# Hybrid decoder block on one core: half of an early query column as three rounded products, and another sequence for the first transfers

## The chip, the cores and the metric

The kernel runs on one core of a Trainium2 chip. The metric is the device time of one launch in microseconds (us). Three runs of the kernel before took 705.67, 705.79 and 706.04 us; the median is 705.79 us. The execution that the profiler recorded took 705.09 us, of which the traced span is 703.3 us.

The engines are called as in the profile: PE multiplies matrices (PEld loads its weights), DVE and ACT work element by element, POOL does small side work and issues some transfers, SP only issues transfers.

## The reference

512 tokens and 16 learned "meta" tokens, 1024 values each, go through a layer norm. One projection of 10,240 columns gives the queries, keys, values and gates of two attention branches. The first branch (8 heads) subtracts two softmaxes with a distance bias, the second (16 heads) is a stick-breaking attention. Gated and merged, they go through an output projection and a last layer norm.

```
h = layer_norm(concat(meta, x), emb_ln_g, emb_ln_b)
lam = exp(sum(lp[0] * lp[1])) - exp(sum(lp[2] * lp[3])) + lam_init
proj = h @ w_in          # q_d k_d v_d g_d q_s k_s v_s g_s m_d m_s
a = softmax(q1 k1 + bias) - lam * softmax(q2 k2 + bias)   # first branch, causal
y_d = rms_norm(a @ v_d);  y_s = stick_breaking(q_s, k_s, v_s)
y = merge(silu(g) * y, sigmoid(m + b_gate)) @ w_out
out = layer_norm(alpha * h + y)[:, 16:]
```

All inputs are float32, and what is computed must keep nearly float32 precision.

## The kernel before, in words

**Rounded products.** Most projections are not made in float32. Each operand is split into a high half (rounded to the faster type fp32r) and a low half (what the rounding lost), and a product is three matmuls into one accumulator: high by high, high by low, low by high. Activations are in `hTh` and `hTl` (transposed: feature rows, token columns; 16 meta columns, then 512). A weight column of 128 outputs is split by `hi` (a cast on ACT, L185) and `lo` (a subtraction on DVE, L190), in two pieces of four feature blocks each; the pieces live in six buffers `w2`. `HALF` names the two halves of the 512 tokens.

**The opening.** Before the high and low halves exist, the kernel loads four tiles of x (`xts`, 128 tokens each), normalizes them (`stats`, `rstd`, `norms`: DVE, POOL, one part on ACT), transposes them on PE (`turn`, L344) and scales them out of the accumulators into `hF` in float32 (`scaled`, L384 on ACT, L386 on DVE). The first two query columns (heads of units 0 and 1) are multiplied in plain float32 from `hF` (`query`, L390): column 0 token block by token block (step `x`), column 1 in two halves of 256 tokens (step `y`). Float32 matmuls need no splits, so PE has work while the splits are made. The first key column and the first value column follow as rounded products over 264 tokens at a time (`proj_pos`, L515).

**What sets the order.** The opening's sequence is written out by hand, as words in a string (L471 to L477): `t` is a transpose, `a` and `d` a scaled copy on ACT or DVE, `s` and `h` the high half on ACT or DVE, `l` the low half, `H` and `L` the halves of a weight column, `N` a normalization, `S` statistics, `x` and `y` query products; `mturn`, `meta`, `hm`, `lm` handle the meta tokens, `lam0` to `lam2` the scalar lambda. The order is then held on PE, DVE, ACT and POOL (`keep_order`). After it, generators (`stage_k`, `stage_v`, `stage_q`, the scores of `d_scores`) are interleaved by `run` according to due times, and a scheduler settles their order on each engine.

**What hangs on lambda.** `lam2` (L453, tile `nlam`) is the last reader of the opening's tile pool. The keys `K`, the constants and the buffers of the attention phase take that memory afterwards, so the first copies of keys (L637 to L642) and POOL's first memset (L595) come behind it.

**Accumulators.** PE writes eight banks: three in pool `pj` (projections), two in `psc` (scores), two in `ptp` (transposes), one in `pav` (values). The two query columns hold two of the `pj` banks until `q_hi` and `q_lo` (L351, L352, L356) have read them. The scores of unit 0 (L764) go to the two `psc` banks in turn, and DVE empties each with the addition of the bias (L844).

**Transfers.** SP issues loads in program order (L257 to L271). The first weight columns go to `raw0` (`first_load`, L133), the later ones to buffers `raw` (L145), which are free again when `lo` has read them. The keys of the following units are stored into place by transfers (L653, L654) on the same queue.

Of the kernel before, what the change touches and what calls it, by code (L numbers as in the profile page):

```python
# [9 lines left out]
F32 = mybir.dt.float32  # L10
# [6 lines left out]
P = 128  # L17
D = 1024
KT = D // P
# [18 lines left out]
WARM = 12  # L38
# [8 lines left out]
def hybrid_block_kernel(ctx: ExitStack, tc: tile.TileContext, x, meta, emb_g, emb_b, w_in, b_gate,  # L47
# [128 lines left out]
    def hi(h):  # L176

        assert len(split) == h
        item = items[h]
        assert not second.get(item)  # L180
        raw = raw0[:, h // 2, ts(h % 2, 4)] if item is None else sums.pop(h) if isinstance(item, tuple) else raws[item]
        w2 = wpool.tile([P, 2, 4, P], F32R, tag="w2", name="w2", bufs=6)
        wh, wl = w2[:, 0], w2[:, 1]
        split.append((raw, wh, wl))
        s.copy(wh, raw)  # L185
# [71 lines left out]
    for i in range(2):  # L257
        for o in (ts(0, 512), ts(1, 512)):
            nc.sync.dma_start(xts[i][:, o], x[0, ts(i, P), o])
# [7 lines left out]
    nc.sync.dma_start(rows2[0:16], b_gate[0].rearrange("a (k p) -> (a k) p", p=P))  # L267
    nc.sync.dma_start(rows2[16:17], subln_g)
# [143 lines left out]
    def norm0():  # L412
        norm_v(0, X0)
        norm_s(0, X1)
        s.copy(cols[:, :16], av0[:, :16])
# [45 lines left out]
    words = dict(lam0=lam0, lam1=lam1, lam2=lam2, hm=lambda: s.copy(hTh[:, :, :M], hM), lm=low_meta, norm0=norm0, mnorm=mnorm, mturn=mturn, meta=meta, more=more_banks,  # L461
                 m0=lambda: stats(4, 0), m1=lambda: stats(4, 1), mr=lambda: rstd(4))

    def order(text):
        for step in text.split():
            if step in words:
                words[step]()
            else:
                steps[step[0]](*map(int, step[1:]))

    order("""S0 norm0 t00 t01 t02 t03 S1 F2 a00 a01 a02 a03 a04 a05 d06 d07 x00 x01 x02 x03 x04 x05 N1 t10 t11 x06 x07 t12 t13  # L471
             a10 a11 a12 a13 a14 a15 a16 a17 S2 m0 m1 mr N2 S3 mnorm
             x10 y00 x11 y01 x12 y02 x13 y03 t20 more t21 t22 t23 x14 y04 x15 y05 x16 y06 x17 y07
             a20 a21 a22 a23 a24 a25 a26 a27 H20 H21 x20 x21 x22 x23 N3 t30 t31 t32 t33 x24 x25 x26 x27 mturn
             a30 a31 a32 a33 a34 a35 a36 a37 x30 x31 x32 x33 x34 x35 x36 x37 y10 y11 y12 y13 y14 y15 y16 y17
             h00 h01 h02 h03 l00 l01 l02 l03 L20 L21 meta h04 h05 h06 h07 l04 l05 l06 l07 hm lm lam0
             s10 s11 s12 s13 l10 l11 l12 l13 s14 s15 s16 s17 l14 l15 l16 l17""")  # L477
    q_hi(0)
    q_lo(0)
    order("H30 H31 lam1 L30 L31 lam2")  # L480
# [25 lines left out]
    def proj_pos(res, kind, i):  # L506
        n = take(kind, i)
        for c in range(2):
            ps = pj.tile([P, 512], F32, tag="pj", name="ps")
# [76 lines left out]
    with tc.tile_pool(name="att", bufs=1) as ap:  # L586
# [379 lines left out]
        run([stage_k(units[0], *UNITS[0], True)], [(2.7, then)])  # L966
# [311 lines left out]
```

## Time and profile before

| what | value |
|---|---|
| median of three runs | 705.79 us |
| the profiled execution | 705.09 us |
| its traced span | 703.3 us |
| PE busy | 693.3 us (99%) |
| DVE busy | 569.5 us (81%) |
| ACT busy | 440.5 us (63%) |
| bytes moved | 124.93 MB |

The busy time of PE is nearly the span; the few us that are missing lie in the opening and at the end. A float32 matmul is recorded as two PE records, a rounded one as one. The start of a record counts, not its length: matmuls overlap, so the time between two starts is what one costs. A row of the timeline gives the start, the time to the end of the last merged record, the engine, the line, the operation and the count.

### The profile page before, as it was taken

Reading aid. Unit: us, or ns where it says so; the run is one execution under the profiler, and the core shown is the slowest. Engines: PE = TensorE matmul, PEld = TensorE weight load, DVE = VectorE, ACT = ScalarE, POOL = GpSimd, SP = SyncE. Lnnn points to the kernel's source line nnn. Section 1 sums busy time; section 2 is a strip of 40 time slices with the busy share of each in tenths; the row PEclk is TensorE's granted clock in tenths of the full one; section 3 lists DMA queues with packets and bytes.
Section 4 is the critical chain, followed back from the end, with each engine's and each line's share of the span. In section 5 each row is a group of like instructions: output and inputs, shape, how many; then the busy total and the mean of one; then the engine's idle time right before and its main releaser. Section 6 shows DMA issues by size and latency. Waiting matters only on the chain.

```text
span 703.3 us, 13282 instructions
## 1 busy us (share of the span) xinstructions
PE 693.3 (99%) x4478; PEld 634.1 (90%) x4478; DVE 569.5 (81%) x1225; ACT 440.5 (63%) x1073; POOL 129.8 (18%) x140
## 2 busy tenths in 40 slices
PE   8999999999999999999999999999999999999996
PEld 8999999989899898999989899988888998999885
DVE  6887998878786777899887898977666888688887
ACT  6676767767566687777757687766555456555400
POOL 2243112222222201212121220000012201230011
PEclk9999999999999999999999999999999999999999
DMA  9399557988888796899898977547477749697702
GB/s 292 103 195 182 145 117 178 212 177 184 221 186 182 188 195 183 173 223 206 207 192 219 203 152 194 164 124 242 137 165 142 148 121 245 136 174 194 264 25 116
DMA packets 184215, 124.93 MB, mean 178 GB/s; under 512 B 8994, under 2 KB 168131, under 8 KB 184147
## 3 DMA queue, kind: packets, MB, share of 16 engines
q1 hardware_dynamic: 148050, 102.84, 50.5%
q0 software_dynamic: 35776, 20.19, 23.0%
q10 hardware_dynamic: 320, 1.06, 0.4%
q8 instruction: 35, 0.57, 0.3%
q14 instruction: 34, 0.27, 0.1%
HBM read 93.54 MB, written 9.44 MB: 146 GB/s over the span
## 4 chain that ended last, share of the span: by engine, by line
PE 93%; ACT 2%; SPq 1%; DVE 1%; DMA 1%; issue 0%; DVEq 0%; ACTq 0%
PE q L700 18%; PE ps L501 12%; PE ps L499 12%; PE ps L500 12%; PE q L1083 11%; PE pso L1206 6%; PE ps L515 6%; PE sc L764 6%; PE t L776 4%; PE tv L733 1%; PE av L931 1%; PE av L932 1%; DMA raw<-in_w_in_dram 1%; PE av L925 1%; PE av L933 1%; DMA xt<-in_x_dram 1%
## 5 line engine op out<-in xcount | busy, mean ns | idle before, releaser
L190 DVE TENSOR_TENSOR w<-raw,w 128x512 fp32r<-128x512 f32 x168 | 114.3, 689 | 37.7 <-ACT w L185 36.4
L500 PE MATMUL ps<-hTl,w 128*128 128x512 f32 x368 | 144.9, 394 | 0.0
L499 PE MATMUL ps<-hTh,w 128*128 128x512 f32 x368 | 144.7, 393 | 0.0
L501 PE MATMUL ps<-hTh,w 128*128 128x512 f32 x368 | 144.7, 393 | 0.0
L185 ACT CAST w<-raw 128x512 fp32r<-128x512 f32 x168 | 103.5, 627 | 11.6 <-PE ps L501 5.4
L147 POOL DMA_DIRECT2D rawk<-in_w_in_dram x48 | 66.1, 1630 | 119.5 <-DMA rawk<-in_w_in_dram 66.1
L700 PE MATMUL q<-tS,w 128*128 128x264 f32 x384 | 82.6, 289 | 0.0
L1083 PE MATMUL q<-gh,w 128*128 128x256 f32 x448 | 81.4, 283 | 0.2 <-ACT t L1092 0.2
L501 PEld LDWEIGHTS ps<-hTh,w 128*128 128x128 f32 x368 | 69.2, 188 | 13.5
L500 PEld LDWEIGHTS ps<-hTl,w 128*128 128x128 f32 x368 | 69.2, 188 | 13.1
L499 PEld LDWEIGHTS ps<-hTh,w 128*128 128x128 f32 x368 | 69.2, 188 | 13.0
L1083 PEld LDWEIGHTS q<-gh,w 128*128 128x128 f32 x448 | 70.2, 192 | 0.5 <-ACT t L1092 0.4
L764 PE MATMUL sc<-k,A 128*128 128x264 f32 (+3 forms) x320 | 66.0, 299 | 0.0
L700 PEld LDWEIGHTS q<-tS,w 128*128 128x128 f32 x384 | 63.7, 189 | 0.3
L1083 PE MATMUL q<-gl,w 128*128 128x256 f32 x224 | 63.5, 283 | 0.0
L700 PE MATMUL q<-hTh,w 128*128 128x264 f32 x288 | 60.8, 286 | 0.0
L916 DVE TENSOR_TENSOR_SCAN e<-e,diag 128x528 f32<-128x528 f32 (+1 forms) x64 | 54.2, 850 | 5.6 <-ACT e L910 5.6
L700 PE MATMUL q<-tl,w 128*128 128x264 f32 x192 | 54.9, 286 | 0.0
L764 PEld LDWEIGHTS sc<-k,A 128*128 128x128 f32 x320 | 50.1, 189 | 2.2
L515 PE MATMUL ps<-hTh,w 128*128 128x264 f32 x256 | 51.5, 289 | 0.2 <-ACT k L642 0.2
L700 PEld LDWEIGHTS q<-hTh,w 128*128 128x128 f32 x288 | 47.8, 189 | 1.0
L781 ACT CAST ah<-t 128x384 fp32r<-128x384 f32 (+2 forms) x72 | 34.3, 477 | 21.7 <-PE t L776 21.6
(284 smaller groups left out, 1572.1 us busy)
## 6 DMA issues: line engine op xcount, KB each, us to landing
raw<-in_w_in_dram SPq DMA_DIRECT2D x142, 256.0 KB, 3.4
rawk<-in_w_in_dram POOLq DMA_DIRECT2D x48, 256.0 KB, 5.7
rawk<-in_w_in_dram SPq DMA_DIRECT2D x36, 256.0 KB, 4.1
k<-ks SPq DMA_DIRECT2D x60, 132.0 KB, 3.0
raw<-in_w_out_dram SPq DMA_DIRECT2D x16, 256.0 KB, 4.0
k<-ks SPq DMA_DIRECT2D x60, 66.0 KB, 2.7
A<-low SPq DMA_DIRECT2D x28, 128.0 KB, 3.1
raw<-in_w_br_diff_dram SPq DMA_DIRECT2D x12, 256.0 KB, 3.3
```

What stands on the lines that cost most here:

```text
L147: second[l] = [lambda raw=raw, x=x: g.dma_start(raw, x, accum_op=ALU.add) for x in more]
L185: s.copy(wh, raw)
L190: eng.tensor_tensor(wl, raw, wh.bitcast(F32), op=ALU.subtract)
L499: pe.matmul(ps, wh[:, k % 4, :], hTh[:, k, M:], start=(k == 0), stop=False)
L500: pe.matmul(ps, wh[:, k % 4, :], hTl[:, k, M:], start=False, stop=False)
L501: pe.matmul(ps, wl[:, k % 4, :], hTh[:, k, M:], start=False, stop=(k == KT - 1))
L515: pe.matmul(ps[:, :H2], a[:, k % 4, :], b[:, k, ts(c, H2)], start=(k == 0 and m == 0), stop=(k == KT - 1 and m == 2))
L700: pe.matmul(bank, a[:, k, :], b, start=start and k == 0 and j == 0, stop=k == 3 and j == 2, skip_group_check=not start)
L764: pe.matmul(ps[:, :n], q, K[:, m, k0:k0 + n], start=(m == 0), stop=(m == 1))
L916: v.tensor_tensor_scan(rev, rev, diag[0][:, L - nk:][:, ::-1], 0.0, ALU.mult, ALU.max)
L1083: pe.matmul(bank, a[:, k, :], b[:, n, k, :], start=start and k == 0 and m == 0, stop=k == 3 and m == 2, skip_group_check=not start)
L1206: pe.matmul(ps, MH[k][:, ts(t, P)] if m == "h" else ML[:, k, ts(t, P)], WO[c]["hl".index(w)][:, k, r], start=(n == 0), stop=(n == 3 * KT - 1))
```

## The change

Four things are done in the opening.

1. The second half (tokens 256 to 511) of the second query column is no longer made in float32 (steps `y10` to `y17`). A new function `first_query` makes it from the split operands, 24 matmuls of 128x256, between the two halves of the first key column. For this the weights of that column are split as well (`H10 H11 L10 L11`).
2. The order of the opening changes: the meta tokens are transposed before the fourth tile, the high halves of the first four feature blocks are cast on ACT earlier (`s00` to `s03` in place of `h00` to `h03`), two low halves move ahead of the last normalization, and lambda moves behind all of it. Two small copies move from ACT to DVE (`cols`, `hm`).
3. The second tile of x is loaded in one transfer, and the small rows (`b_gate`, `subln_g`) directly behind it.
4. The second half of the first key column is accumulated in the bank of `pav` instead of a third `pj` bank.

```
-WARM = 12
+WARM = 13
...
-        split.append((raw, wh, wl))
+        split[h:h + 1] = [(raw, wh, wl)]
...
-    for i in range(2):
-        for o in (ts(0, 512), ts(1, 512)):
-            nc.sync.dma_start(xts[i][:, o], x[0, ts(i, P), o])
+    for o in (ts(0, 512), ts(1, 512)):
+        nc.sync.dma_start(xts[0][:, o], x[0, ts(0, P), o])
+    nc.sync.dma_start(xts[1], x[0, ts(1, P), :])
+    nc.sync.dma_start(rows2[0:16], b_gate[0].rearrange("a (k p) -> (a k) p", p=P))
+    nc.sync.dma_start(rows2[16:17], subln_g)
     first_load(0, ts(0, 4))
...
-        s.copy(cols[:, :16], av0[:, :16])
+        v.tensor_copy(cols[:, :16], av0[:, :16])
...
-             a10 a11 a12 a13 a14 a15 a16 a17 S2 m0 m1 mr N2 S3 mnorm
+             a10 a11 a12 a13 a14 a15 a16 a17 s00 s01 s02 s03 S2 m0 m1 mr N2 S3 mnorm l00 l01
...
+             L20 L21 meta hm lm l02 l03 h04 h05 h06 h07 l04 l05 l06 l07 L10 L11 l10 l11 l12 l13 l14 l15 l16 l17""")
     q_hi(0)
     q_lo(0)
-    order("H30 H31 lam1 L30 L31 lam2")
+    order("H30 H31 L30 L31 lam0 lam1 lam2")
+
+    def first_query():
+        for k in range(KT):
+            _, wh, wl = split[2 + k // 4]
+            for m, (a, b) in enumerate(((wh, hTh), (wh, hTl), (wl, hTh))):
+                pe.matmul(pss[1][:, 256:], a[:, k % 4, :], b[:, k, HALF[1]], start=(k == 0 and m == 0),
+                          stop=(k == KT - 1 and m == 2))
...
-            ps = pj.tile([P, 512], F32, tag="pj", name="ps")
+            ps = (pj if n > 4 or c == 0 else pav).tile([P, 512], F32, tag="pj" if n > 4 or c == 0 else "av", name="ps")
...
-        run([stage_k(units[0], *UNITS[0], True)], [(2.7, then)])
+        run([stage_k(units[0], *UNITS[0], True)], [(2.5, first_query), (2.7, then)])
```

PE, from the transpose of the fourth tile (`xn_105`) to the first key column (`w_312`), before:

```order
L344 MATMUL bank<-ident,xn_105 128x128 x8
L390 MATMUL bank<-hF,raw_87 128x128 x4
L424 MATMUL bank<-ident,mn 128x16 x8
L425 MATMUL bank<-ident,small 128x17
L390 MATMUL bank<-hF,raw_87 128x128 x8
L390 MATMUL bank<-hF,raw_87 128x256 x8
L515 MATMUL ps<-hTh,w_312 128x264
```

The same place now (the first key column's weights are `w_318`):

```order
L423 MATMUL bank<-ident,mn 128x16 x8
L424 MATMUL bank<-ident,small 128x17
L343 MATMUL bank<-ident,xn_105 128x128 x8
L389 MATMUL bank<-hF,raw_87 128x128 x12
L520 MATMUL ps<-hTh,w_318 128x264
```

The eight float32 matmuls of 128x256 are gone from here, and the key column stands directly behind the products of the first query column. On PE where the first half of the key column (`w_320`) is done, now:

```order
L520 MATMUL ps<-hTl,w_320 128x264
L520 MATMUL ps<-hTh,w_320 128x264
L484 MATMUL bank<-hTh,w_350 128x256
L484 MATMUL bank<-hTl,w_350 128x256
L484 MATMUL bank<-hTh,w_350 128x256 x2
```

Here the 24 rounded matmuls of 128x256 (weights `w_350` and `w_368`) are inserted; the second half of the key column follows them.

DVE, up to lambda (`nlam`), before (`hTl` are low halves of activations, `A` the queries, `w` low halves of weights):

```order
L401 TENSOR_TENSOR hTl<-hF,hTh 128x256 x8
L356 SCALAR_TENSOR_TENSOR A_172<-bank,A_171 64x512
L356 SCALAR_TENSOR_TENSOR A_171<-bank,A_171 64x512
L190 TENSOR_TENSOR w_412<-raw_87,w_412 128x512
L190 TENSOR_TENSOR w_414<-raw_87,w_414 128x512
L453 TENSOR_SCALAR nlam<-lexp 128x1
```

The same place now:

```order
L189 TENSOR_TENSOR w_350<-raw_87,w_350 128x512
L189 TENSOR_TENSOR w_368<-raw_87,w_368 128x512
L400 TENSOR_TENSOR hTl<-hF,hTh 128x256 x8
L355 SCALAR_TENSOR_TENSOR A_172<-bank,A_171 64x512
L355 SCALAR_TENSOR_TENSOR A_171<-bank,A_171 64x512
L189 TENSOR_TENSOR w_408<-raw_87,w_408 128x512
L189 TENSOR_TENSOR w_410<-raw_87,w_410 128x512
L445 ISA lscr,lsum<-small 128x64
L445 ISA lsum 128x1
L445 ISA lscr,lsum<-small 128x64
L445 ISA lsum 128x1
L452 TENSOR_SCALAR nlam<-lexp 128x1
```

Two more weight subtractions stand ahead of lambda, and its two sums stand right in front of it, where they stood ahead of the eight low halves before.

PE behind the first value column (`w_414`), before (`sc` are scores of unit 0: `k_442` and `k_443` are the keys of its two components, `w_544` the weights of the next key column):

```order
L515 MATMUL ps<-hTh,w_414 128x264
L764 MATMUL sc<-k_442,A_171 128x264 x2
L764 MATMUL sc<-k_443,A_172 128x264 x2
L515 MATMUL ps<-hTh,w_544 128x264
L515 MATMUL ps<-hTl,w_544 128x264
L515 MATMUL ps<-hTh,w_544 128x264 x2
```

The same place now:

```order
L520 MATMUL ps<-hTh,w_410 128x264
L769 MATMUL sc<-k_440,A_171 128x264 x2
L769 MATMUL sc<-k_441,A_172 128x264 x4
L769 MATMUL sc<-k_440,A_171 128x400 x2
L520 MATMUL ps<-hTh,w_566 128x264
L520 MATMUL ps<-hTl,w_566 128x264
L769 MATMUL sc<-k_441,A_172 128x400 x2
L520 MATMUL ps<-hTh,w_566 128x264 x2
```

Four groups of scores now stand there without projection matmuls between them, where two stood; a fifth follows two matmuls later.

DVE at the scores now (`e` empties a bank of scores):

```order
L849 ISA e_438,mn<-sc,bias 128x264
L849 ISA mn 128x1
L646 TENSOR_TENSOR k_441<-ps,k_441 64x264
L849 ISA e_438,mn<-sc,bias 128x264
L849 ISA mn 128x1
L849 ISA e_439,mn<-sc,bias 128x264
L849 ISA mn 128x1
L852 TENSOR_TENSOR mn<-mn 128x1
L849 ISA e_439,mn<-sc,bias 128x264
L849 ISA mn 128x1
L189 TENSOR_TENSOR w_566<-raw,w_566 128x512
```

Before, the two subtractions of the next key column's weights stood directly behind the copy `k_443`, ahead of the second `e`; now the first of them (`w_566`) comes behind the fourth. From the next value column on, the order on every engine is the old one.

## Rows read from the trace of the kernel before

**Rows 1.** The page, parts 1 and 4: busy time by engine, and the ending chain
```profile
PE 693.3 (99%) x4478; PEld 634.1 (90%) x4478; DVE 569.5 (81%) x1225; ACT 440.5 (63%) x1073; POOL 129.8 (18%) x140
...
PE 93%; ACT 2%; SPq 1%; DVE 1%; DMA 1%; issue 0%; DVEq 0%; ACTq 0%
```

**Rows 2.** Waits of PE over the span: total us, times, longest us
```profile
PE ps L515 <- ACT k L642: 0.2, 1, 0.2
```

**Rows 3.** Timeline of PE, 23 to 34 us: start us, us, instruction [idle before]
```profile
23.00 3.62 PE L390 MATMUL bank<-hF,raw 128*128 128x256 f32 x16
26.27 0.47 PE L515 MATMUL ps<-hTh,w 128*128 128x264 f32 x1
...
32.14 0.28 PE L515 MATMUL ps<-hTh,w 128*128 128x264 f32 x1
32.26 0.58 PE L764 MATMUL sc<-k,A 128*128 128x264 f32 x2
33.05 0.39 PE L515 MATMUL ps<-hTh,w 128*128 128x264 f32 x1 [0.21 <-ACT k L642]
```

**Rows 4.** The ending chain, rounded matmuls of 128x256: start us, us, count
```profile
538.45 40.31 PE q L1083 x336
```

**Rows 5.** Timeline of DVE, 17 to 31 us
```profile
17.12 1.00 DVE L340 TENSOR_SCALAR xn<-xt,xmv,xrs 128x512 f32<-128x512 f32 x2 [0.71 <-POOL xrs L300]
18.04 0.89 DVE L396 CAST hTh<-hF 128x256 fp32r<-128x256 f32 x4
18.85 1.43 DVE L401 TENSOR_TENSOR hTl<-hF,hTh 128x256 fp32r<-128x256 f32 x4
...
24.07 0.28 DVE L434 TENSOR_TENSOR hTl<-hM,hTh 128x128 fp32r<-128x128 f32 x1
...
24.68 2.77 DVE L401 TENSOR_TENSOR hTl<-hF,hTh 128x256 fp32r<-128x256 f32 x8
...
28.92 1.29 DVE L190 TENSOR_TENSOR w<-raw,w 128x512 fp32r<-128x512 f32 x2
30.13 0.21 DVE L453 TENSOR_SCALAR nlam<-lexp 128x1 f32<-128x1 f32 x1
```

**Rows 6.** Timeline of ACT, 14 to 38 us
```profile
14.63 2.90 ACT L384 ACTIVATE hF<-bank,cols 128x128 f32<-128x128 f32 x8 [1.05 <-PE bank L344]
17.38 1.18 ACT L185 CAST w<-raw 128x512 fp32r<-128x512 f32 x2
...
22.24 2.55 ACT L396 CAST hTh<-hF 128x256 fp32r<-128x256 f32 x8
...
30.50 0.37 ACT L637 CAST k<-ps 64x264 fp32r<-64x264 f32 x1 [3.03 <-DVE nlam L453]
...
32.63 0.38 ACT L642 CAST k<-ps 64x264 fp32r<-64x264 f32 x1 [0.50 <-DVE k L641]
...
37.46 0.38 ACT L642 CAST k<-ps 64x264 fp32r<-64x264 f32 x1 [0.50 <-DVE k L641]
```

**Rows 7.** Timeline of the opening, DVE and PE
```profile
7.01 1.28 DVE L323 BATCH_NORM_STATS2 lnst<-xt 128x6 f32<-128x512 f32 x2
...
9.54 1.00 DVE L340 TENSOR_SCALAR xn<-xt,xmv,xrs 128x512 f32<-128x512 f32 x2 [0.40 <-POOL xrs L300]
...
10.27 0.60 PE L344 MATMUL bank<-ident,xn 128*128 128x128 f32 x4
```

**Rows 8.** Timeline at the first scores (DVE) and the next unit's (SP, PE)
```profile
36.08 0.41 DVE L844 CUSTOM_DVE_ANT_0 e<-sc,bias 128x264 f32<-128x264 f32 x1
...
38.39 1.31 DVE L190 TENSOR_TENSOR w<-raw,w 128x512 fp32r<-128x512 f32 x2 [0.96 <-ACT w L185]
...
53.46 0.62 SPq L653 DMA_DIRECT2D k<-ks  x1
...
59.44 0.40 PE L764 MATMUL sc<-k,A 128*128 128x264 f32 x2
```

**Rows 9.** Transfers between 38 and 62 us: count, KB each, median us to landing
```profile
k<-ks SPq DMA_DIRECT2D x4, 132.0 KB, 4.7
```

More of the change, by code (lines that the diff above doesn't have):

```diff
@@ L176, in hi @@
     def hi(h):
-        assert len(split) == h
         item = items[h]
@@ L266, in hybrid_block_kernel @@
     first_load(2)
-    nc.sync.dma_start(rows2[0:16], b_gate[0].rearrange("a (k p) -> (a k) p", p=P))
-    nc.sync.dma_start(rows2[16:17], subln_g)
     first_load(3)
@@ L460, in hybrid_block_kernel @@
     steps["H"], steps["L"] = lambda n, c: hi(2 * n + c), lambda n, c: lo(2 * n + c)
-    words = dict(lam0=lam0, lam1=lam1, lam2=lam2, hm=lambda: s.copy(hTh[:, :, :M], hM), lm=low_meta, norm0=norm0, mnorm=mnorm, mturn=mturn, meta=meta, more=more_banks,
+    words = dict(lam0=lam0, lam1=lam1, lam2=lam2, hm=lambda: v.tensor_copy(hTh[:, :, :M], hM), lm=low_meta, norm0=norm0, mnorm=mnorm, mturn=mturn, meta=meta, more=more_banks,
                  m0=lambda: stats(4, 0), m1=lambda: stats(4, 1), mr=lambda: rstd(4))
@@ L471, in hybrid_block_kernel @@
     order("""S0 norm0 t00 t01 t02 t03 S1 F2 a00 a01 a02 a03 a04 a05 d06 d07 x00 x01 x02 x03 x04 x05 N1 t10 t11 x06 x07 t12 t13
-             a10 a11 a12 a13 a14 a15 a16 a17 S2 m0 m1 mr N2 S3 mnorm
+             a10 a11 a12 a13 a14 a15 a16 a17 s00 s01 s02 s03 S2 m0 m1 mr N2 S3 mnorm l00 l01
              x10 y00 x11 y01 x12 y02 x13 y03 t20 more t21 t22 t23 x14 y04 x15 y05 x16 y06 x17 y07
[L474 to L477, printed above, removed]
+             a20 a21 a22 a23 a24 a25 a26 a27 H20 H21 x20 x21 x22 x23 N3 mturn t30 t31 t32 t33 x24 x25 x26 x27
+             H10 a30 a31 a32 a33 a34 a35 a36 a37 x30 x31 x32 x33 x34 x35 x36 x37 H11 s10 s11 s12 s13 s14 s15 s16 s17
+             L20 L21 meta hm lm l02 l03 h04 h05 h06 h07 l04 l05 l06 l07 L10 L11 l10 l11 l12 l13 l14 l15 l16 l17""")
     q_hi(0)
     q_lo(0)
-    order("H30 H31 lam1 L30 L31 lam2")
+    order("H30 H31 L30 L31 lam0 lam1 lam2")
[5 more added lines that the diff above has]
+                          stop=(k == KT - 1 and m == 2))
     def then():
```

## The prediction

> **What bounds the kernel now.** I read the page first: PE is busy for 693.3 of 703.3 us, and the chain that ended last runs over PE for 93% of the span [rows 1]. So a change in the opening is worth what it does to PE's sequence there: matmul time that goes, and waits that come or go. Then the waits of PE: over the whole run only one is listed between the first microseconds and the last third, 0.2 us for ACT's copy of the keys [rows 2]. That row is short because it counts only time without a running record. The timeline of PE shows the real one: two score matmuls start at 32.26, and the next matmul starts at 33.05 [rows 3]. Rounded matmuls follow each other every 0.120 us (336 of them in 40.31 us) [rows 4], so PE was ready at 32.26 + 0.24 = 32.50 and lost 0.55 us. Last I read DVE and ACT ahead of that wait. ACT's copy at 30.50 had waited 3.03 us for lambda, which DVE made at 30.13, and DVE's rows leave hardly a gap from 18.04 to there [rows 5, 6]. So two things stand beside each other here: PE's own work, and a chain DVE, lambda, key copies, scores. The change shortens the first and moves the second.
>
> **The column in rounded products.** From 23.00 to 32.26 PE made eight float32 matmuls of 128x256 (16 records) and 48 rounded ones [rows 3]. The 48 cost 48 x 0.120 = 5.76 us, which leaves 9.26 - 5.76 = 3.50 us for the eight. The 24 that replace them cost 24 x 0.120 = 2.88 us, a price that is measured for this very shape [rows 4]. PE saves 0.62 us, all on the path. The other PE steps (transposes of the meta tokens, the fourth tile) change places only.
> The Trainium skill's page "TensorE: Matmul & The Clock Gate", section "Back-to-back issue gap", gives 262 cycles at 2.4 GHz for 256 columns, 109 ns. By that, an estimate from the page, the 24 would cost 2.62 us and the saving would be 0.88. The trace does not agree, 120 ns, and the sum goes by the trace.
>
> **Do its operands come in time?** If not, the saving is only moved. The first key half now starts where the float32 matmuls did, near 23.0, and ends 24 x 0.12 = 2.9 later, near 25.9; the query's matmuls then want one low half of the tokens 256 to 511 every 0.36 us. DVE makes one every 0.35 (eight in 2.77) [rows 5]. Before, the first of them started at 24.68; now two weight subtractions stand ahead, but four casts and two low halves have left. By the balance below the first is ready near 25.1 to 25.5. PE meets each some 0.5 us after it is made. I count no wait; a bound is 0.3.
>
> **The second tile in one transfer, a copy moved to DVE.** DVE's statistics of that tile start at 7.01 with no idle time before them; their result reaches PE as transposes at 10.27, behind a normalization at 9.54 that waited for POOL [rows 7]. The first of its two normalizations ends near 10.04 (half of 1.00 after 9.54), so PE is bound by its own work there with about 0.2 us to spare. Now the small copy `cols` stands ahead of the statistics, and they must wait for the whole tile. Both halves had landed by 7.65, when the second half's statistics began (half of 1.28 after 7.01). So the delay is between 0 and 0.64 us; I take 0.15 to 0.25, of which PE feels 0.05. Bounds for PE: 0 and 0.45. From there PE runs without a wait, so this passes on.
> What the Trainium skill says ("DMA: Bandwidth & Descriptors", section "Anatomy of one DMA") speaks against this part: the semaphore fires only when the last byte of a transfer has landed. The rows agree that a half could be used alone (statistics from 7.01 on), but also that the DVE was not waiting for it.
>
> **Lambda, and what follows it.** On DVE, from 18.04 to lambda at 30.13: four casts go to ACT (18.04 to 18.85, 0.81 less) and two low halves move into the 0.71 us in which DVE waited at 17.12 (2 x 0.35 = 0.70 less). Two weight subtractions are added (28.92 to 30.13, 1.21) and the cast `hm` (0.20, the nearest row is the subtraction of the same size at 24.07, between 0.2 and 0.3) [rows 5]. So DVE has about 0.1 us less work. But three hand-overs that were covered are not now. The first weight subtraction needs ACT's cast, which started at 17.38; ACT now makes four casts (0.32 each, 2.55 for eight) ahead of the copies at 14.63, where it had been idle for 1.05 [rows 6], so it is 0.23 late, done near 18.2. That is a wait of 0.15. The meta transposes come to 0.1. And the two sums of lambda stand in front of it with nothing between, so DVE waits for ACT's exponential: between 0.2 (its own time alone) and the 0.71 of the row at 17.12, I take 0.35. With 0.2 from the opening, lambda comes -0.1 + 0.15 + 0.1 + 0.35 + 0.2 = 0.7 us later (bounds 0.3 and 1.2).
> The key copies hang on it. ACT's last of the first half ended at 33.01, of the second at 37.84 [rows 6]; now 33.7 and 38.55.
> PE in these times: the second key half ends at 32.26 - 0.62 + 0.05 = 31.69. The first half of the value column follows at once (another bank, free since the first query was read): 34.57. Scores, 34.81. The second half of the value column needs the bank that ACT frees at 33.7: no wait, 37.69. The old 0.55 is gone. Then come four groups of scores in a row. Two need 0.48 us, 38.17. The third of them needs the last key copy at 38.55, so PE waits to 38.6: 0.45. Its successor needs a bank that DVE empties with the third `e`, and two of them at 0.41 [rows 8] behind the key subtraction (about 38.15) end near 39.0: 0.15 more. And the first low-half weight matmul needs the subtraction `w_566`, which DVE makes behind the fourth `e`: 39.55 + 0.65 = 40.2, where PE arrives at 39.95: 0.3 more. In sum PE waits 0.9 where it waited 0.55: 0.35 lost. With lambda at its bounds this is between -0.1 and 0.85.
>
> **The weights and keys behind it.** The subtractions that stood at 38.39 [rows 8] now come near 40, so the buffers `raw` are free some 1.5 us later and SP's loads go out later; behind them on SP stand the stores of the next unit's keys. The fourth pair of these was issued at 53.46 and such a store needs 4.7 us in this stretch, landing near 58.2; PE wants the scores at 59.44 [rows 8, 9]. That is 1.3 us to spare against a shift of 1.5: I take 0.15, bounds 0 and 0.6. The weights themselves are loaded for later columns; they cost nothing while that is so.
>
> **Sum.** -0.62 + 0.05 + 0.35 + 0.15 = -0.07 us, so 705.0 for the profiled execution of 705.09. The median of the runs is 0.70 above it; I forecast 705.79 - 0.07, rounded 705.7 us. With all bounds low it is -0.7, with all high 1.3.
>
> **Rivals.**
> *The saving is kept in full.* If DVE loses nothing at the hand-overs, or the scores wait for nothing, the old wait of 0.55 is gone too: -0.62 - 0.55 = -1.17, 704.6 us; half kept, 705.2. For it: PE's value column fills the time in which the keys are copied. Against it: four groups of scores share two banks, and DVE empties one in 0.41 us while PE fills one in 0.24.
> *The stores of the keys end last.* At 59.44 the first scores of unit 1 wait for transfers. Price: if loads and stores shift by as much as three `e` and three subtractions in front of the first freed buffers (3 x 0.41 + 3 x 0.65 = 3.2 us), less the 1.3 to spare, 1.9 us, so about 707.5 with the rest of the sum. It decides from a shift of 1.3 us on; slower than the 0.2% bound needs 2.8. For it: this queue issues in order and the stretch's transfers are slow (4.7). Against it: the queue has no gap to lose, so an issue that is later need not land later by as much.
> *The opening's front.* If the second tile counts with its upper bound 0.45, and lambda with its own 1.2, the sum is -0.62 + 0.45 + 0.85 + 0.15 = 0.8, 706.6 us.
>
> **How the numbers follow.** Forecast (705.4 to 706.3) 0.52; saving kept (704.5 to 705.4) 0.24; opening's front (706.3 to 707.0) 0.12; stores last (from 706.9 on) 0.12. What this measurement tells from no change is 0.2%, 1.41 us: below 704.38 or above 707.20. Even the full saving of 1.17 stays inside; faster gets 0.04. Of the stores' case three quarters lie beyond, slower gets 0.09, and no measurable change 0.87. The range is 704.7 to 706.9: it holds the forecast, nearly all of the saving kept and most of the opening's front.
>
> **What would show it.** Right: in the new trace 24 rounded matmuls of 128x256 every 0.12 us between the two halves of the first key column, without a gap; lambda 0.5 to 1 us later than 30.13; no wait ahead of the value column's second half; then PE gaps of about 0.9 us in sum in front of the scores and the next key column. Wrong in the column: gaps inside the 24, with DVE's low halves as releaser. Wrong in the chain: lambda not later, or PE reaching the next key column with under 0.3 us lost. Wrong behind: a gap at the scores of unit 1 with a transfer `k<-ks` as releaser. Wrong in front: the transposes at 10.27 moved by over 0.2 us.

## The result, and the profile after

The changed kernel took 706.39 us (median of 22 runs, 705.53 to 708.11), the kernel before 705.76 us (22 runs). The ratio is 1.0013, 95% interval 1.0007 to 1.0019: about 0.6 us (0.09%) slower. That lies in the forecast range (704.7 to 706.9) and inside the 0.2% called "no measurable change", but on the other side of no change than the forecast of -0.07 us, and the interval leaves it no doubt. The profiled execution took 706.26 us, its span is 704.5 us.

The page, parts 1 and 4, answers to [rows 1]. PE is still busy nearly all the time; of POOL and DVE more in a moment.

```profile
PE 694.7 (99%) x4488; PEld 635.3 (90%) x4488; DVE 570.9 (81%) x1225; ACT 442.2 (63%) x1077; POOL 131.2 (19%) x140
...
PE 95%; ACT 2%; DVE 2%; issue 1%; POOL 0%; DVEq 0%; POOLq 0%; ACTq 0%
```

The waits of PE, against [rows 2]: the wait for the key copy (L642) is gone, and a new one stands in its place.

```profile
PE sc L769 <- DVE mn L849: 0.7, 1, 0.7
```

As before, such a row counts only time without a running record. The timeline of PE in the opening shows the whole; it answers to [rows 3] and to the PE rows of [rows 7] and [rows 8].

```profile
7.00 0.23 PE L312 MATMUL cp<-ident,rows 16*128 16x16 f32 x1
...
10.49 0.66 PE L343 MATMUL bank<-ident,xn 128*128 128x128 f32 x4
...
23.29 0.37 PE L520 MATMUL ps<-hTh,w 128*128 128x264 f32 x1
...
26.29 0.28 PE L484 MATMUL bank<-hTh,w 128*128 128x256 f32 x1
...
29.15 0.29 PE L520 MATMUL ps<-hTh,w 128*128 128x264 f32 x1
...
34.95 0.40 PE L769 MATMUL sc<-k,A 128*128 128x264 f32 x2
...
37.96 0.28 PE L520 MATMUL ps<-hTh,w 128*128 128x264 f32 x1
38.13 0.76 PE L769 MATMUL sc<-k,A 128*128 128x264 f32 x4
39.56 0.90 PE L769 MATMUL sc<-k,A 128*128 128x264 f32 x4 [0.67 <-DVE mn L849]
40.29 0.28 PE L520 MATMUL ps<-hTh,w 128*128 128x264 f32 x1
40.41 0.28 PE L520 MATMUL ps<-hTl,w 128*128 128x264 f32 x1
40.58 0.64 PE L769 MATMUL sc<-k,A 128*128 128x400 f32 x2
41.18 0.51 PE L520 MATMUL ps<-hTh,w 128*128 128x264 f32 x2
...
60.01 0.64 PE L769 MATMUL sc<-k,A 128*128 128x264 f32 x4
```

Read it from the top. The second tile's transposes start at 10.49 where they started at 10.27: 0.22 lost. The first key column starts at 23.29, where the float32 matmuls stood at 23.00: 0.29 lost by now. The 24 rounded matmuls run from 26.29 to 29.15, 2.86 us without a gap; the eight float32 ones had cost 3.50. From there to the last matmul of the value column (37.96; in the kernel before it started at 38.83) there is no wait, and the old one of 0.55 us is gone. Here the changed kernel leads by 0.87 us. Then it loses all of that: from 37.96 to the third matmul of the next key column (41.18) pass 3.22 us, in which PE has 1.80 us of work (nine matmuls of 264 columns at 0.12 and four of 400 at 0.18). The difference, 1.42 us, is waiting. At the scores of unit 1 it is 60.01 against 59.44: 0.57 us behind, and that is the result.

DVE in the same stretch answers to [rows 5] and [rows 7]:

```profile
7.26 0.17 DVE L414 COPY cols<-cp 128x16 f32<-128x16 f32 x1 [0.16 <-PE cp L312]
7.36 1.27 DVE L322 BATCH_NORM_STATS2 lnst<-xt 128x6 f32<-128x512 f32 x2
...
9.88 1.00 DVE L339 TENSOR_SCALAR xn<-xt,xmv,xrs 128x512 f32<-128x512 f32 x2 [0.42 <-POOL xrs L299]
...
16.59 0.74 DVE L400 TENSOR_TENSOR hTl<-hF,hTh 128x256 fp32r<-128x256 f32 x2
18.05 1.00 DVE L339 TENSOR_SCALAR xn<-xt,xmv,xrs 128x512 f32<-128x512 f32 x2 [0.72 <-POOL xrs L299]
...
31.54 0.21 DVE L452 TENSOR_SCALAR nlam<-lexp 128x1 f32<-128x1 f32 x1 [0.27 <-ACT lexp L449]
```

Lambda comes at 31.54, 1.41 us later than before, twice what was forecast. Its delay has three pieces. At the second tile's normalization (9.88 against 9.54) it is 0.34. At the fourth tile's (18.05 against 17.12) it is 0.93, so 0.59 came in between. From there to lambda it took 13.01 us and now 13.49, another 0.48. The middle piece is the surprising one: two low halves stand at 16.59, where DVE used to wait 0.71 us for POOL, and yet DVE still waits 0.72 us behind them. POOL's rows say why, first the kernel before, then the changed one:

```profile
15.82 0.64 POOL L299 TENSOR_TENSOR lne<-xmv,epsr 128x1 f32<-128x1 f32 x1 [1.11 <-DVE xmv L327]
16.54 0.55 POOL L300 TENSOR_TENSOR xrs<-lne,neghalf 128x1 f32<-128x1 f32 x1
```

```profile
16.08 1.31 POOL L298 TENSOR_TENSOR lne<-xmv,epsr 128x1 f32<-128x1 f32 x1 [1.11 <-DVE xmv L326]
17.47 0.55 POOL L299 TENSOR_TENSOR xrs<-lne,neghalf 128x1 f32<-128x1 f32 x1
```

The addition to 128 numbers takes 0.19 us elsewhere in these traces. Here it lasts until DVE's row of instructions has ended (16.46 before, the meta tokens' normalization ending at 16.41; 17.39 now, the second low half ending at 17.33). What DVE puts into its wait for POOL holds up the POOL it waits for.
The Trainium skill's page "SBUF — State Buffer", section "Who interferes with whom", bears on this: a VectorE instruction with two operands in SBUF, as these subtractions are, contends with a GpSimd instruction that reads SBUF, because its second operand comes through the read interface that the two engines share. The trace agrees, with 1.31 us against 0.64, and it shows that POOL did not get in between the instructions of the row.

The key copies on ACT, against [rows 6], start 1.53 us later (32.03 against 30.50), and the last of them ends at 39.35 against 37.84:

```profile
31.30 0.20 ACT L449 ACTIVATE lexp<-lsum 128x2 f32<-128x2 f32 x1 [3.22 <-DVE lsum L445]
...
32.03 0.37 ACT L642 CAST k<-ps 64x264 fp32r<-64x264 f32 x1
...
38.98 0.38 ACT L647 CAST k<-ps 64x264 fp32r<-64x264 f32 x1 [0.50 <-DVE k L646]
```

What ended PE's wait can be read more closely, from DVE and from PE's weight loads at the same place:

```profile
38.51 0.43 DVE L646 TENSOR_TENSOR k<-ps,k 64x264 fp32r<-64x264 f32 x1 [0.49 <-ACT k L645]
38.97 0.43 DVE L849 CUSTOM_DVE_ANT_0 e<-sc,bias 128x264 f32<-128x264 f32 x1
39.33 0.08 DVE L849 DVE_READ_ACCUMULATOR2_ANT mn<- 128x1 f32 x1
...
39.53 0.59 PEld L769 LDWEIGHTS sc<-k,A 128*128 128x128 f32 x4 [0.86 <-ACT k L647]
...
41.18 0.30 PEld L520 LDWEIGHTS ps<-hTh,w 128*128 128x128 f32 x2 [0.30 <-DVE w L189]
```

The third group of scores behind the value column (39.56) needs the last key copy and a free bank. The copy ended at 39.35; the bank was emptied by the `e` that stands on DVE behind the key subtraction, at 39.41, and it is DVE that PE's row names. Both follow the same subtraction (38.51). Up to the third group PE lost 1.00 of the 1.42 us; the other 0.42 lie behind its start, at the next banks and at the weights `w_566`, which DVE splits behind the fourth `e` (41.18).

### The profile page after: what moved, and what is told of

It is laid out like the page before. It is cut to its first block, busy times and chain, and to the rows that moved or that the text cites. A ratio compares the mean times of both kernels' runs of the same rounds, so it can differ in the third digit from the quotient of the medians.

```text
span 704.5 us, 13302 instructions
## 1 busy us (share of the span) xinstructions
PE 694.7 (99%) x4488; PEld 635.3 (90%) x4488; DVE 570.9 (81%) x1225; ACT 442.2 (63%) x1077; POOL 131.2 (19%) x140
## 4 chain that ended last, share of the span: by engine, by line
PE 95%; ACT 2%; DVE 2%; issue 1%; POOL 0%; DVEq 0%; POOLq 0%; ACTq 0%
PE q L705 18%; PE ps L505 12%; PE ps L506 12%; PE ps L504 12%; PE q L1088 11%; PE pso L1211 6%; PE sc L769 6%; PE ps L520 5%; PE t L781 4%; PE tv L738 1%; PE bank L389 1%; PE warm L308 1%; PE av L936 1%; PE av L937 1%; PE av L930 1%
## 5 line engine op out<-in xcount | busy, mean ns | idle before, releaser
L189 DVE TENSOR_TENSOR w<-raw,w 128x512 fp32r<-128x512 f32 x170 | 115.9, 690 | 36.8 <-ACT w L184 35.7
```

Source lines behind the costliest of these rows:

```text
L189: eng.tensor_tensor(wl, raw, wh.bitcast(F32), op=ALU.subtract)
```

## The experiments

Theory 1: PE's new wait is the lateness of the last key copy behind the end of the value column, and that copy hangs on the chain DVE, lambda, copies. Rival: four groups of scores in a row on two banks set the wait, whenever lambda comes. All kernels are the changed one with an edit, except where said. The times of each kernel stand beside runs of the kernel before, taken together with it on the same chip.

| kernel | median us | before | ratio to before (95%) | lambda | C: last key copy ends | V: last value matmul | C - V | PE's wait |
|---|---|---|---|---|---|---|---|---|
| before | 705.76 | | | 30.13 | 37.84 | 38.83 | -0.99 | 0 |
| changed | 706.39 | 705.76 | 1.0013 (1.0007 to 1.0019) | 31.54 | 39.35 | 37.96 | 1.39 | 1.42 |
| e1 | 706.69 | 705.55 | 1.0018 (1.0009 to 1.0027) | 31.68 | 39.50 | 37.85 | 1.65 | 1.68 |
| e2 | 706.33 | 705.55 | 1.0008 (1.0000 to 1.0017) | 31.49 | 39.31 | 37.98 | 1.33 | 1.36 |
| e3 | 705.85 | 705.55 | 1.0005 (0.9997 to 1.0014) | 31.52 | 39.21 | 38.33 | 0.88 | 0.96 |
| e4 | 706.00 | 705.55 | 1.0008 (0.9999 to 1.0017) | 28.21 | 38.80 | 37.78 | 1.02 | 1.05 |
| e5 | 705.92 | 705.68 | 1.0004 (0.9995 to 1.0012) | 30.57 | 38.38 | 38.79 | -0.41 | 0 |
| e6 | 705.72 | 705.68 | 1.0001 (0.9992 to 1.0010) | 31.10 | 37.07 | 37.78 | -0.71 | 0 |
| e7 | 704.63 | 705.68 | 0.9986 (0.9977 to 0.9995) | 31.20 | 37.17 | 37.90 | -0.73 | 0 |
| e8 | 705.07 | 705.68 | 0.9992 (0.9983 to 1.0001) | 28.09 | 36.59 | 37.72 | -1.13 | 0 |
| e9 | 706.57 | 705.76 | 1.0015 (1.0006 to 1.0024) | 32.70 | 40.51 | 39.56 | 0.95 | 0.98 |
| e10 | 705.71 | 705.76 | 1.0001 (0.9992 to 1.0010) | 32.17 | 38.14 | 38.84 | -0.70 | 0 |
| e11 | 706.22 | 705.80 | 1.0006 (0.9997 to 1.0015) | 30.18 | 37.88 | 38.88 | -1.00 | 0 |
| e12 | 705.07 | 705.80 | 0.9990 (0.9981 to 0.9999) | 30.78 | 36.75 | 37.65 | -0.90 | 0 |

Lambda, C and V are times in each profiled execution (V is the start of the matmul). The wait is the time from V to the third matmul of the next key column, less 1.80; a 0 says that the matmuls behind V follow without a gap of over 0.2 us. Single executions begin up to 0.3 us apart, since the first tile lands at other times, so C - V and the wait are read within one trace. Times are compared by the ratios, since the kernel before itself took 705.55 to 705.80 us beside them. Wherever C lies behind V, the wait is C - V plus 0.03 to 0.08 us; wherever it lies ahead, there is none. Within the six kernels that have a wait it moves with C - V one for one, so the lateness of the key chain sets its length; that speaks for theory 1.

Two things limit this. First, in these six the third group of scores starts 0.15 us after DVE has emptied its bank, in each; after the last key copy it starts 0.21 us in five and 0.26 in e3, where the emptying came 0.05 later. So the bank ends the wait, a link behind the key subtraction that theory 1 did not have, and 0.42 us of the wait lie behind that start in all six. The rival's banks have their part, but not "whenever lambda comes". Second, in the eight kernels without a wait the scores also stand in another order: two groups directly behind V, the third 2.3 to 4.1 us after it. No run has early copies with four groups in a row, so that early copies alone end the wait is not shown.

**e1: the two low halves behind the normalization.**

```
-mnorm l00 l01
+mnorm
-L20 L21 meta hm lm l02
+L20 L21 meta hm lm l00 l01 l02
```

> The changed kernel with one edit: the two low halves that it put in DVE's wait for POOL's reciprocal root (ahead of the fourth tile's normalization) stand behind that normalization again. Theory 1 (the wait can't be filled so: POOL's first small addition does not get through while DVE runs subtractions of two SBUF operands, so they pushed the root back by their own 0.67 us): POOL's addition takes 0.64 us again instead of 1.31, the fourth tile's normalization starts near 17.4 instead of 18.05, lambda stays within 0.15 us of 31.54, and the time is that of the changed kernel within 0.3 us. Rival (the low halves did use the wait, and lambda is late for another reason): the addition stays at 1.31 us, lambda is 0.6 to 0.7 us later, and the time 0.4 to 0.7 us longer than the changed kernel's.

POOL's timeline in e1, the same row as above:

```profile
16.09 0.64 POOL L298 TENSOR_TENSOR lne<-xmv,epsr 128x1 f32<-128x1 f32 x1 [1.11 <-DVE xmv L326]
```

The addition is back at 0.64 us and the normalization starts at 17.39, so the hold-up is shown. Lambda is at 31.68. In both kernels the meta tokens' normalization starts at 15.92, so the two can be compared from there: the fourth tile's comes 0.66 us earlier in e1, and lambda 0.14 later, within the 0.15 expected. So the place in the wait was worth 0.14 us, and not the 0.70 that the two low halves cost by themselves. The median is 0.3 us longer, but the two intervals overlap, so that is not shown.

**e2: the copy cols on ACT, e9: cp ahead of the warm-up.**

```
-        v.tensor_copy(cols[:, :16], av0[:, :16])
+        s.copy(cols[:, :16], av0[:, :16])
```

> The changed kernel with one edit: the small copy cols is back on ACT. Theory 1 (the front of the opening lost 0.28 us to this copy, which stands ahead of DVE's statistics and waits for PE's transposes): the statistics of the second tile start at 7.0 to 7.15 instead of 7.36, PE's transposes of it at 10.25 to 10.35 instead of 10.49, lambda is 0.2 to 0.35 us earlier, and the time is 0.2 to 0.35 us shorter than the changed kernel's. Rival (the second tile in one transfer is what came late): the statistics still start near 7.3, and the time is the changed kernel's within 0.1 us.

With the copy on ACT the statistics follow the first normalization after 0.45 us (6.86, 7.31), as before (0.45); in the changed kernel it was 0.80. By the ratios the kernel is 0.05% (0.35 us) shorter than the changed one, as expected, but the two intervals overlap, so the size is not shown. What the copy costs varies: it waits for cp, which stands behind all warm-up matmuls, and these take 0.21 us a record up to a certain moment and 0.11 from then on, which fits the clock's two levels (1.2 and 2.4 GHz). The windows of the profile print a granted clock of 1.00 for both stretches; but the first entry of the granted clock in the trace, at the higher level, stands within 0.1 us of that moment wherever the moment falls inside the warm-up (6.64 us in the changed kernel). In the thirteen profiles with the warm-up in one piece it lies between 4.5 and 7.5 us. The change also makes the warm-up two records longer (`WARM = 13`), so cp comes 0.2 to 0.4 us later; no run takes that apart. Where the copy is on DVE, the second tile's transposes followed the first normalization by 3.67 us at best (e1, e4, e6) and by 4.46 at worst (e3); with the copy on ACT and one transfer by 3.71 always (e2, e7, e8). So e9 took cp out from behind the warm-up:

```
-    fill(WARM)
     av0 = pav.tile([P, 512], F32, tag="av", name="cp")
+    fill(6)
     pe.transpose(av0[:, :16], rows, ident[:16, :16])
+    fill(WARM - 6)
```

> The changed kernel with PE's small transposes cp moved ahead of the last seven warm-up matmuls; the copy cols stays on DVE. Theory 1 (the front loses time because the copy waits for transposes that stand behind all warm-up matmuls, and these take 0.21 us a record while PE's clock is still at its lower level): cp is done before 5.5 us whenever the clock rises, DVE's first normalization is followed by the copy and the statistics without a wait (statistics 0.5 to 0.6 us after the normalization's start, not 0.80), PE's transposes of the second tile come 3.6 to 3.75 us after it (3.93 in the changed kernel), and the time is 0.1 to 0.4 us shorter than the changed kernel's. Rival (the copy itself or the transfer in one piece costs it): still 3.9 us, no change.

PE's timeline in e9, the warm-up and the first tile's transposes:

```profile
1.43 2.93 PE L308 MATMUL warm<-ident 128*128 128x128 f32 x12 [1.43 <-POOL ident masks.py:199]
4.78 0.26 PE L312 MATMUL cp<-ident,rows 16*128 16x16 f32 x1 [0.42 <-DMA rows<-in_emb_ln_b_dram]
4.96 3.36 PE L308 MATMUL warm<-ident 128*128 128x128 f32 x14
8.11 1.91 PE L344 MATMUL bank<-ident,xn 128*128 128x128 f32 x8
```

DVE did go on without a wait (normalization 6.63, statistics 7.17). But cp had to wait 0.42 us for its rows, and behind this break PE stayed at the slower spacing until 10.9 us, where the trace's first entry of the clock stands: 14 warm-up records in 3.36 us, and eight transposes in 1.91 us that took 1.09 before. The second tile's transposes came at 12.15. The kernel was no faster, and the expectation failed for a reason that neither theory had. This execution took 707.6 us, 1.0 above the kernel's median, so what other executions lose there is not shown.

**e3, e4: lambda earlier.** In e3 the sums and the exponential stand where they stood before the change, in e4 all of lambda stands ahead of the last weight subtractions.

```
-meta hm lm l02
+meta hm lm lam0 l02
-H30 H31 L30 L31 lam0 lam1 lam2
+H30 H31 lam1 L30 L31 lam2
```

> The changed kernel with one edit: lambda's two sums and the exponential stand where they stood before the change (the sums ahead of the low halves, the exponential ahead of the last weight subtractions), only the last subtraction lam2 stays behind the value column's weights. Theory 1 (PE's wait of 1.4 us at the scores follows lambda): DVE no longer waits for ACT's exponential, lambda comes 0.3 to 0.4 us earlier (near 31.2), PE waits some 0.3 us less before the second key column, and the time is 0.2 to 0.4 us shorter than the changed kernel's. Rival (the wait is that of four groups of scores in a row on two banks, whenever lambda comes): PE waits 1.3 to 1.5 us there as before, and the time is the changed kernel's within 0.15 us.

PE's wait fell by 0.46 us, somewhat more than the 0.3 expected; the rival would have left it. The time, by the ratios, fell by 0.56, but the two intervals overlap.

```
-meta hm lm l02
+meta hm lm lam0 lam1 l02
-l16 l17
+l16 l17 lam2
-H30 H31 L30 L31 lam0 lam1 lam2
+H30 H31 L30 L31
```

> The changed kernel with all three steps of lambda moved ahead of the query's low half and the value column's weight subtractions, so that the last reader of the opening's memory is done near 28.5 us instead of 31.54. Theory 1 (the key copies and with them PE's wait at the scores hang on that last reader): ACT's first key copy starts near 28.7 instead of 32.03; the subtractions of the keys on DVE then follow the value column's weights at about 31.2 instead of 32.44, the last key copy ends about 1.2 us earlier than 39.36, PE's wait of 1.4 us at the scores shrinks to 0.3 to 0.8, and the time is 0.5 to 1.1 us shorter than the changed kernel's. Rival (the scores' order and their two banks set the wait): the wait stays above 1.2 us, and the time is the changed kernel's within 0.2 us.

ACT's timeline in e4, the first two key copies:

```profile
28.57 0.37 ACT L642 CAST k<-ps 64x264 fp32r<-64x264 f32 x1 [0.16 <-DVE nlam L452]
31.87 0.37 ACT L644 CAST k<-ps 64x264 fp32r<-64x264 f32 x1 [2.93 <-DVE k L643]
```

The first copy starts 3.5 us earlier, the second waits 2.93 us for DVE's subtraction of the keys, which stands behind the value column's weights. Lambda 3.3 us earlier was worth 0.4: it was the head of the chain only until DVE's own work was. The wait shrank, but less than forecast (1.05, not 0.3 to 0.8), and so did the time (0.35 us by the ratios, not 0.5 to 1.1).

**e5: the column in float32 again, all else as changed.**

```
-H10 a30
+a30
...
-x34 x35 x36 x37 H11
+x34 x35 x36 x37 y10 y11 y12 y13 y14 y15 y16 y17
-L10 L11 l10
+l10
-[(2.5, first_query), (2.7, then)]
+[(2.7, then)]
```

> The changed kernel with its first part undone: the second half of the second query column is made in float32 again, between the first query column and the first key column, and its weights are not split (two casts on ACT and two subtractions on DVE less); all else as changed. Theory 1 (PE's wait follows the last key copy, and the two weight subtractions are 1.2 us of the DVE chain to it): the eight float32 matmuls cost PE 3.5 us instead of 2.9, lambda comes 0.9 to 1.3 us earlier, the last key copy is done before the value column ends, so PE's wait of 1.4 us at the scores falls to 0 to 0.4; in sum the time is 0.4 to 0.8 us shorter than the changed kernel's, though PE has 0.6 us more work. Rival (the column's saving stands by itself, the wait is that of the scores' order): the time is 0.5 to 0.7 us longer than the changed kernel's.

By the ratios 0.6 us shorter than the changed kernel, with 0.6 us more work on PE. The two weight subtractions (1.2 us on DVE) are gone, lambda is at 30.57 although this execution began 0.24 later, and C lies ahead of V. The two intervals overlap (this one reaches up to 1.0012, the changed kernel's down to 1.0007), and the scores stand in the other order here, so the wait of 1.42 us is gone for two reasons at once. Still, the change stands here in one experiment: the rounded column gives PE 0.64 us and takes 1.2 from the engine on which PE waits next.

**e6, e7, e8: the copies of the keys first.** With lambda as in e3, ACT reads the second query column ahead of the key copies (where it waits for lambda) and not between their halves. e7 has the edit of e2 as well; e8 has those of e2 and e4 in place of e3's.

```
-[(2.5, first_query), (2.7, then)]
+[(2.5, first_query), (2.55, lambda: q_hi(1)), (2.7, lambda: q_lo(1))]
```

> The changed kernel with lambda's sums and exponential where they stood before, and ACT's reading of the second query column (two copies, 1.2 us) moved from between the two halves of the key copies to ahead of them, where ACT waits for lambda anyway. Theory 1 (PE's wait is the lateness of the last key copy behind the end of the value column): the key copies of the second half follow the first half at once, the last one is done 1.5 to 2.5 us earlier than 39.35, ahead of the end of the value column, and PE's wait falls from 1.4 us to 0 to 0.4; the time is 0.8 to 1.5 us shorter than the changed kernel's. The places of the scores behind the first four matmuls change too, since the scheduler counts with the earlier copies. Rival (two banks and DVE's emptying set the wait): a wait of 0.7 us or more stays, and the time is at most 0.5 us shorter.

In e6, ACT's timeline (the second query column, then the last copy of the first half, the first and last of the second), and PE's behind the value column:

```profile
29.17 0.60 ACT L350 ACTIVATE A<-bank 128x512 fp32r<-128x512 f32 x1 [0.82 <-PE bank L484]
...
33.52 0.38 ACT L647 CAST k<-ps 64x264 fp32r<-64x264 f32 x1 [0.50 <-DVE k L646]
33.92 0.37 ACT L642 CAST k<-ps 64x264 fp32r<-64x264 f32 x1
...
36.69 0.38 ACT L647 CAST k<-ps 64x264 fp32r<-64x264 f32 x1 [0.50 <-DVE k L646]
```

```profile
37.78 0.28 PE L520 MATMUL ps<-hTh,w 128*128 128x264 f32 x1
37.90 0.64 PE L769 MATMUL sc<-k,A 128*128 128x264 f32 x4
38.38 0.29 PE L520 MATMUL ps<-hTh,w 128*128 128x264 f32 x1
```

The copies end at 37.07, and PE goes through the scores without a wait. The scheduler, which counts with earlier copies, also puts fourteen projection matmuls ahead of the third group of scores behind V, so this run does not part the copies from the order. At the scores of unit 1 this execution is at 58.57, 0.87 us ahead of the kernel before. By the ratios it is 0.12% (0.85 us) shorter than the changed kernel, with intervals that overlap a little, and equal to the kernel before.

> As the kernel with the key copies first (lambda's sums early, the second query column read ahead of the key copies), and the small copy cols back on ACT. Theory 1: another 0.1 to 0.4 us shorter than that kernel, because DVE's statistics of the second tile no longer wait for PE's small transposes behind the warm-up matmuls; in sum 1.0 to 1.7 us shorter than the changed kernel, and 0.4 to 1.1 us shorter than the kernel before. Rival (the copy costs nothing): equal to the kernel with the key copies first within 0.1 us.

> As the kernel with the key copies first and cols on ACT, but with all three steps of lambda ahead of the last weight subtractions, so that the key copies wait for nothing but PE and DVE. Theory 1: the last key copy was already ahead of the end of the value column, so nothing more is won: equal to the kernel with the key copies first and cols on ACT within 0.2 us. Rival (lambda itself still holds something, or an earlier start of the copies shifts the scores to better places): 0.3 us or more shorter.

e7 is the fastest kernel here: 704.63 us, 0.14% below the kernel before. e8 did not beat it, as expected, though it was 0.4 us longer where at most 0.2 was expected; the intervals overlap. e7 is 1.1 us below e6, far more than the 0.1 to 0.4 expected of the copy; here too the intervals overlap a little (0.9995 and 0.9992), the lowest of twelve kernels may have come out low, and at the scores of unit 1 the two profiled executions are level (58.64 and 58.57). That other executions of e6 lose more at cp than its profiled one (0.11 us a record from 4.9 us on, no wait) would fit, and it was not shown.

**e10, e11, e12: the transfers.** e10 is e7 with the second tile in halves (the diff below), e12 is e7 with part 3 of the change undone, e11 is the kernel before with part 3 alone.

```
-    nc.sync.dma_start(xts[1], x[0, ts(1, P), :])
+    for o in (ts(0, 512), ts(1, 512)):
+        nc.sync.dma_start(xts[1][:, o], x[0, ts(1, P), o])
```

> The kernel with the key copies first and cols on ACT, with the second tile of x loaded in two halves again (the small rows stay where the change put them). Theory 1 (the transfer in one piece has landed before DVE asks for it, so it costs nothing): the statistics follow the first normalization at once in both, and the time is that of the kernel with the key copies first and cols on ACT within 0.25 us. Rival (the whole tile is late in many executions): 0.3 us or more shorter.

The expectation failed: 1.1 us longer than e7. SP's timeline shows it, e7 first (its third tile of x), then e10:

```profile
2.97 0.95 SPq L133 DMA_DIRECT2D raw<-in_w_in_dram  x2
3.96 0.50 SPq L263 DMA_DIRECT2D xt<-in_x_dram  x1
```

```profile
3.45 0.94 SPq L133 DMA_DIRECT2D raw<-in_w_in_dram  x2
4.91 0.35 SPq L264 DMA_DIRECT2D xt<-in_x_dram  x1
```

Of e10 one row of SP's waits, and one of DVE's timeline:

```profile
SPq L264 <- DMA xt<-in_x_dram: 0.5, 1, 0.5
```

```profile
13.18 1.27 DVE L323 BATCH_NORM_STATS2 lnst<-mt 16x6 f32<-16x512 f32 x2 [0.61 <-DMA mt<-in_meta_tokens_dram]
```

The ninth issue waits until an earlier transfer has landed, and with the halves and the early small rows this ninth is the third tile, 0.95 us later; what stands behind it comes later too: DVE waits 0.61 us for the meta tokens, and PE 0.45 at 12.78 for weights.

> The kernel with the key copies first and cols on ACT, with the whole old sequence of transfers (second tile in halves, small rows late). Theory 1 (what cost the kernel with the halves 1 us is that one more issue stood ahead of the third tile, which then had to wait for a landing at 4.9 us): with the small rows late again the third tile is issued near 3.6 us, the fourth tile's normalization comes near 18.1 us as with the new sequence, not 19.0, and the time is that of the kernel with the key copies first and cols on ACT within 0.3 us. Rival (the halves themselves cost it): about 1 us longer than that kernel, as with the halves and the early rows.

With the small rows late the third tile goes out at 3.63, and the time is e7's within its error (ratios 0.9990 and 0.9986). So neither piece alone shows a cost; halves and early rows together do, by 1.1 us, with intervals that overlap a little (0.9992 and 0.9995).

> The kernel before with the changed sequence of transfers alone (second tile in one transfer, the two small rows directly behind it). Theory 1 (an issue waits until an earlier transfer has landed once several are out; the sequence is worth only what PE, bound by its own work from 10.3 us on, feels of it): the third tile is issued within 0.4 us of 3.63, PE's timeline from 10.27 on is the old one, and the time is that of the kernel before within 0.3 us. Rival (the sequence itself makes the opening faster or slower): 0.4 us or more off.

In the kernel before the new sequence does nothing to the opening: the scores of unit 1 stand at 59.48 (59.44). Its median is 0.4 us higher, a little over the 0.3 expected, with an interval that holds 1. The trace has 0.69 us more in one wait at 492.9 us (a value matmul for ACT's copy `af`), which other kernels have with other lengths.

## Why the prediction was wrong

The steps, by their own names:

- **The column in rounded products** (-0.62): right. 24 matmuls in 2.86 us, -0.64.
- **Do its operands come in time** (no wait): right, no gap inside the 24.
- **The second tile in one transfer, a copy moved to DVE** (+0.05): mis-sized. 0.22 at the transposes, 0.29 at the key column. The forecast looked at the transfer and gave the copy no wait of its own; the transfer cost nothing (e2), the copy waited 0.16 us for cp and took its time ahead of the statistics. This size is that of one execution: from the first normalization to these transposes it is 3.93 us here, 3.71 before, and 3.67 to 4.46 in the edited kernels with the copy on DVE and the warm-up in one piece.
- **Lambda, and what follows it** (+0.7 later, PE waits 0.9): the step that failed. Its sum took 0.70 us off DVE because "two low halves move into the 0.71 us in which DVE waited". They did not fit: POOL, for which DVE waited, was held up by them, and 0.59 of the 0.70 came back as delay (e1: their place was worth 0.14). Together with 0.34 from the front instead of 0.2, lambda came 1.41 us later. What was forecast behind the fourth tile (0.5: the casts, the weight subtractions, three uncovered hand-overs) came to 0.48. The step from the copies to PE was right in kind. What it counted behind the start of the third group of scores (0.15 for a bank, 0.3 for the weights) came to 0.42. The wait ahead of it was 1.00 and not 0.45: the last key copy ended at 39.35 and not at 38.55, and the emptying of the bank, for which the forecast had only the next group wait, ended it 0.06 later still. So PE waited 1.42 us and not 0.9, and lost 0.87 against the old 0.55, not 0.35.
- **The weights and keys behind it** (+0.15): nothing. From the next column of 512 (53.35, now 53.93) to the scores of unit 1 it takes 6.08 us, 6.09 before.

With the measured sizes the sum is 0.29 - 0.64 - 0.55 + 1.42 = 0.52, beside 0.57 in the trace and 0.63 in the medians. Luck kept the miss from being larger: front and lambda were off by 0.24 and 0.52 the same way, and the 0.15 for the weights, which came to nothing, hid part of it. The other 0.6 us by which the two spans differ arise at about 400 us and behind; waits there (0.63 us for a key store at 402.1 in e7, 1.07 for ACT at 494.3 in e1, none of both in the kernel before) come and go from one profile to the next, and what sets them stayed open.

Of the rivals, "the saving is kept in full" comes nearest to what e7 has, once ACT's reading of the column no longer stands between the key copies (and the scores stand in another order). "The stores of the keys end last" did not happen in the changed kernel; PE waits for such stores in e6 and e7 (0.5 us at 131.6, 0.6 at 402.1), far behind the place that was named. "The opening's front" was the nearest in time, with lambda even past its upper bound of 1.2.

## What to carry to other kernels

Work moved into an engine's wait is free only if it does not slow the engine that is waited for: before counting a wait as a place, look at what the releaser reads and how long its own small instructions last beside such work. When a change takes matmul time and pays with work on the engine that feeds the next stage, follow that chain to the next instruction at which PE waits for it (here the key copies, and the bank that is emptied behind them, against the end of the value column), and count both at that place. Where the gain was eaten there, moving the copies forward, with the order of scores that followed from it, gave it back (e7); a cheaper PE column alone did not.

## What the runs showed that was not expected

- In the one profile of e9, PE kept to 0.21 us a record until 10.9 us behind a 0.42 us break in its warm-up, and the second tile's transposes came 1.7 us later than in the changed kernel. That the break was the cause fits and rests on this one execution.
- The moment at which the warm-up's records go from 0.21 to 0.11 us varies from 4.5 to 7.5 us between executions; an instruction that waits for PE in that time takes the variation into the time.
- POOL's addition on 128x1 took 0.19 us beside DVE's statistics and 1.31 us beside a row of three DVE instructions on SBUF, without getting in between them.
- The third group of scores followed the emptying of its bank by 0.15 us in six kernels, although the weight load beside it names the last key copy: two things that hang on one instruction look alike until one run sets them 0.05 us apart (e3).
- The first transfers: one issue more ahead of a tile moved that tile by 0.95 us, through a wait for an earlier landing.
